# FFN and layer activations turned by VectorE and DMA instead of by TensorE, in a float32 decoder layer on one Trainium2 core

## The chip, the cores and the metric

One of the eight cores of a Trainium2 chip runs the program. The metric is the device time of one execution in microseconds (us). A core has five engines: TensorE (matmuls; PE in the profile, PEld its weight loads), VectorE (DVE), ScalarE (ACT), GpSimd (POOL) and SyncE (SP, which here only issues DMAs). Each engine takes its instructions in program order; a DMA is issued from an engine's queue and waits there for what it depends on.

## What is computed

The reference is one decoder layer over 256 positions with 2048 channels, in float32. Cut to what matters here:

```python
h = x + 0.5 * swiglu(rms_norm(x, norm_ffn1), w1_gate, w1_up, w1_down)       # D_FF = 5632
z = rms_norm(h, norm_mix) @ w_in
y = concat(rms_norm(s5_mixer(z_ssm)), rms_norm(gmlp_mixer(z_u, z_v)))
h = h + y @ w_out
h = h + 0.5 * swiglu(rms_norm(h, norm_ffn2), w2_gate, w2_up, w2_down)
h = h + sigmoid(rms_norm(h, norm_ple) @ w_ple_gate) * (p @ w_ple_proj)
return rms_norm(h, norm_final)
# swiglu(x) = (silu(x @ w_gate) * (x @ w_up)) @ w_down;  g below is the bracket
```

## The kernel before

Everything is a stream of weight products. `ffn_groups`, `mix_groups` and `ple_groups` write a plan of groups; a group is 512 output columns of one weight matrix, for both halves t of the 256 positions, summed over its blocks k of 128 rows. `stream` (L94) walks the plan in steps of two blocks, called ticks here: `load` (L108) issues a 1 MB weight load on SP for every two ticks, with three buffers `raw`; `do_split` (L117) splits a tick's weights into a high part `wh` (ScalarE, L133) and a low part `wl` (VectorE, L134), three ticks ahead of their use, with four buffers each; `products` (L138) issues the tick's 12 matmuls (2 blocks, 2 halves, 3 products at L147, L148 and L149) into a PSUM tile `acc`. A group over 2048 rows has 8 ticks, one over 5632 rows (w_down) has 22, and one over 1024 rows (w_out) has 4.

When a group's last tick is issued, its `post` is spawned and runs at once (L166 to L168). A post is a generator: `yield n` puts what follows n ticks later, so the order of every engine's queue is set by where a post stands among the ticks. The posts that matter here:

- `up_post` (L365), after each of the 11 pairs of a gate group and an up group of an FFN (one pair is 16 ticks): VectorE multiplies (L371, two instructions) into the tile `g`; then, one and two ticks later, four 128x128 blocks of g are transposed by TensorE into a PSUM tile `tr` (`transposes`, L196 to L200), and `split_plain` (L202) splits this into `gTah`/`gTal` or `gTbh`/`gTbl` (ScalarE L203, VectorE L204). These are the stationary operands of w_down.
- `down_post` (L387), after each of the four groups of w_down: VectorE adds into h (L390), ScalarE squares it (`square`, L223), and `h_to_T` (L225) transposes the 512 columns in two steps of four blocks, one and two ticks later, and splits them with the gain of the next norm (`split_gain2`, L211: ScalarE L214, VectorE L217) into `hTh`/`hTl`, the stationary operands of the next stage.
- `wo_post` (L863), after each of the four last groups of w_out: the same with L867 in place of L390.

So four blocks are transposed 44 times for g (11 pairs, 2 FFNs, 2 steps) and 24 times for h (12 chunks of 512 columns, 2 steps). Other transposes (`s5_tables`, `s5_block`, `gmlp`, `glu_post`) use the same helper.

Beside FFN1 runs `s5_tables` (L431), a long chain of small VectorE work that is paced by a budget per tick (`paced`, L67). It is cut into four quarters. In each, GpSimd clears two columns of the tile `qt` (`g.memset`, L606 and L607) right before VectorE fills the table (L608 and L525), and `put` (L527) stores it to DRAM (`stash`) by DMA. GpSimd also computes each norm's power (`rstd`, L194) and part of `s5_block` (L687). It issues no DMA.

Of the kernel before, what the change touches and what calls it, by code (L numbers as in the profile page):

```python
# [7 lines left out]
F32 = mybir.dt.float32  # L8
F32R = mybir.dt.float32r
I32 = mybir.dt.int32  # L10
AF = mybir.ActivationFunctionType
# [4 lines left out]
P = 128  # L16
# [5 lines left out]
NW = 512  # L22
# [32 lines left out]
class Layer:  # L55
# [166 lines left out]
        j = self.junk_p.tile([P, NW], F32, tag="junk", name="junk")  # L222
        self.nc.scalar.activation(out=j, in_=src, func=AF.Square, accum_out=acc)  # L223

    def h_to_T(self, n, gcol):  # L225

        for b in range(2):
            yield 1
            k0 = 4 * n + 2 * b
            ps = self.transposes(  # L230
                [self.h[:, t, (k0 + kk) * P:(k0 + kk + 1) * P] for kk in range(2) for t in range(2)])
            self.split_gain2(ps, self.gcol[:, gcol + k0:gcol + k0 + 2], self.hTh[:, k0:k0 + 2], self.hTl[:, k0:k0 + 2])
# [4 lines left out]
    def kernel(self):  # L237
        tc, nc, I = self.tc, self.nc, self.i
        pool = tc.tile_pool
        base = [pool(name="const", bufs=1), pool(name="small", bufs=2), pool(name="raw", bufs=3),  # L240
                pool(name="wh", bufs=LA_SPLIT + 1), pool(name="wl", bufs=LA_SPLIT + 1), pool(name="junk", bufs=1),
                pool(name="acc", bufs=4, space=PSUM), pool(name="aux", bufs=4, space=PSUM),
                pool(name="dram", bufs=1, space=DRAM)]
        const, self.small, self.raw_p, self.wh_p, self.wl_p, self.junk_p, self.acc_p, self.aux_p, dram = [
            p.__enter__() for p in base]
        self.gcol = const.tile([P, 96], F32, name="gcol")
        nc.scalar.dma_start(out=self.gcol, in_=I["cols"])
        self.ident = const.tile([P, P], F32, name="ident")
        make_identity(nc, self.ident)
        self.mhalf = const.tile([P, 2], F32, name="mhalf")  # L250
        nc.gpsimd.memset(self.mhalf, -0.5)
        act_warm = const.tile([P, 2], F32, name="act_warm")
        nc.scalar.activation(out=act_warm, in_=self.mhalf, func=AF.Silu)
        self.mag2 = const.tile([P, 32], F32, name="mag2")
        self.r = [const.tile([P, 2], F32, name=f"r{n}") for n in range(6)]
        self.ssq = [const.tile([P, 4, 2], F32, name=f"ssq{n}") for n in range(7)]
        self.h = const.tile([P, 2, D], F32, name="h")
        self.hTh = const.tile([P, 16, 256], F32R, name="hTh")
        self.hTl = const.tile([P, 16, 256], F32R, name="hTl")
        self.stash = dram.tile([2 * NQ, P, BW], F32, name="stash")  # L260
        self.pools, self.cms = {}, {}

        self.plan = []
        self.ffn_groups(1)
        self.mix_groups()
        self.ffn_groups(2)
        self.ple_groups()


        warm = self.aux_p.tile([P, NW], F32, tag="aux", name="warm")  # L270
        for _ in range(N_WARM):
            nc.tensor.matmul(warm[:, 0:P], self.ident, self.ident, start=True, stop=True)
        self.open("gta", "gt")
        self.open_g()
        self.open("xt", "xt")
        xt = self.pools["xt"].tile([P, 16, 256], F32, name="xt")
        self.preload, self.presplit = {}, {}

        def xt_load(a, b):
            return lambda: nc.sync.dma_start(out=xt[:, a:b, :], in_=I["xT"][:, a:b, :])  # L280

        def x_load(t):
            return lambda: nc.sync.dma_start(out=self.h[:, t, :], in_=I["x"][:, t, :])

        def xt_split(i):
            def f():
                for k in ((i,) if i < 2 else (2 * i - 2, 2 * i - 1)):
                    self.split_gain(xt[:, k, :], self.gcol[:, k:k + 1], self.hTh[:, k, :], self.hTl[:, k, :])
                if i == 8:
                    self.close("xt")  # L290
            return f
        for li, fs in {0: [xt_load(0, 1)], 1: [xt_load(1, 2)], 2: [xt_load(2, 4)], 3: [xt_load(4, 6)],
                       4: [xt_load(6, 8)], 5: [xt_load(8, 12)], 6: [xt_load(12, 16)], 7: [x_load(0)],
                       8: [x_load(1)]}.items():
            self.preload[li] = fs
        for i in range(9):
            self.presplit[i] = [xt_split(i)]

        def startup():
            yield 6  # L300
            for t in range(2):
                for n in range(4):
                    self.square(self.h[:, t, n * NW:(n + 1) * NW], self.ssq[0][:, n, t:t + 1])
                    if n % 2:
                        yield 1
            self.rstd([self.ssq[0][:, n, :] for n in range(4)], D, self.r[0])
        self.spawn(startup())
        self.spawn(self.paced(self.s5_tables()), 8)
        self.stream()
        for n in list(self.pools)[::-1]:  # L310
            self.close(n)
        for p in base[::-1]:
            p.__exit__(None, None, None)
# [11 lines left out]
    KA = 24  # L325

    def open_g(self):
        self.gT_a = (self.pools["gta"].tile([P, self.KA, 256], F32R, name="gTah"),
                     self.pools["gta"].tile([P, self.KA, 256], F32R, name="gTal"))
        self.open("gs", "gs", 2)  # L330

    def open_gb(self):
        self.open("gtb", "gtb")
        n = 44 - self.KA
        self.gT_b = (self.pools["gtb"].tile([P, n, 256], F32R, name="gTbh"),
                     self.pools["gtb"].tile([P, n, 256], F32R, name="gTbl"))

    def gT_at(self, k):
        if k < self.KA:
            return self.gT_a, k  # L340
        return self.gT_b, k - self.KA

    def ffn_groups(self, which):
        I = self.i
# [19 lines left out]
        def up_post(c):  # L364
            def post(g):  # L365
                gt = st.pop(c)
                if which == 1 and c == 6:
                    self.close("wrk")
                    self.open_gb()
                for t in range(2):  # L370
                    self.nc.vector.scalar_tensor_tensor(  # L371
                        out=gt[t], in0=g.ps[t], scalar=r[:, t:t + 1], in1=gt[t], op0=ALU.mult, op1=ALU.mult)
                for b in range(2):
                    yield 1
                    ps = self.transposes(
                        [gt[t][:, (2 * b + kk) * P:(2 * b + kk + 1) * P] for kk in range(2) for t in range(2)])
                    (th, tl), k = self.gT_at(4 * c + 2 * b)
                    self.split_plain(ps, th[:, k:k + 2, :].rearrange("p a b -> p (a b)"),
                                     tl[:, k:k + 2, :].rearrange("p a b -> p (a b)"))
            return post  # L380

        def act_g(k, t):
            (th, tl), kk = self.gT_at(k)
            return th[:, kk, t * P:(t + 1) * P], tl[:, kk, t * P:(t + 1) * P]

        def down_post(n):
            def post(g):  # L387
                for t in range(2):
                    hs = self.h[:, t, n * NW:(n + 1) * NW]
                    self.nc.vector.scalar_tensor_tensor(  # L390
                        out=hs, in0=g.ps[t], scalar=0.5, in1=hs, op0=ALU.mult, op1=ALU.add)
                ssq = self.ssq[1 if which == 1 else 5]
                for t in range(2):
                    self.square(self.h[:, t, n * NW:(n + 1) * NW], ssq[:, n, t:t + 1])
                if n == 3:
                    self.rstd([ssq[:, i, :] for i in range(4)], D, self.r[1 if which == 1 else 4])
                yield from self.h_to_T(n, 16 if which == 1 else 48)
            return post

        for c in range(11):  # L400
# [393 lines left out]
    def mix_groups(self):  # L794
# [68 lines left out]
        def wo_post(n, rr, ssm):  # L863
            def post(g):
                for t in range(2):
                    hs = self.h[:, t, n * NW:(n + 1) * NW]
                    nc.vector.scalar_tensor_tensor(out=hs, in0=g.ps[t], scalar=rr[:, t:t + 1], in1=hs,  # L867
                                                   op0=ALU.mult, op1=ALU.add)
                if not ssm:
                    return  # L870
                for t in range(2):
                    self.square(self.h[:, t, n * NW:(n + 1) * NW], self.ssq[4][:, n, t:t + 1])
                if n == 3:
                    self.rstd([self.ssq[4][:, i, :] for i in range(4)], D, self.r[3])
                yield from self.h_to_T(n, 32)
            return post

        def glu_post(n):
# [218 lines left out]
```

## Time and profile before

| | us |
|---|---|
| three runs, median | 1879.89 (1879.21 to 1880.82) |
| the profiled execution, its own time | 1880.12 |
| the span of its instructions in the trace | 1878.4 |
| granted TensorE clock over the span | 0.999 of full speed |

The profile is one execution. Its page gives the busy time of each engine, the chain of work that ended last (followed back from the last instruction, at each step to what released it), the costliest groups of instructions by line, engine and tile, and the DMA issues. The trace can also be asked for the instructions in order of time, for waits, and for busy time by stretch. Matmuls are pipelined: a row's duration is longer than the time from its start to the next one's start.

### The profile page before, as it was taken

To read this page: it belongs to the slowest core of one execution; us is meant where nothing else is said; L and a number is where in the kernel's file an instruction comes from. 1 tells how busy PE (TensorE), PEld (TensorE's weight loads), DVE (VectorE), ACT (ScalarE), POOL (GpSimd) and SP (SyncE) were. 2 spreads that over 40 slices of the span, in tenths; PEclk is the share of its full clock that TensorE was granted. 3 is DMA by queue.
4 is the path that set the end of the run, shared out by engine and by line. 5 is a ranking of instruction groups with operands and counts; after the bars stand their busy time and mean duration, and the time that the engine had idled before them with its cause. 6 is when DMAs were issued, how large, how long until landed. Compare 5 with 4: busy or idle time off the path is not lost.

```text
span 1878.4 us, 21983 instructions
## 1 busy us (share of the span) xinstructions
PE 1866.7 (99%) x8752; PEld 1549.8 (83%) x8752; DVE 1115.5 (59%) x1519; ACT 845.4 (45%) x1018; POOL 45.9 (2%) x58
## 2 busy tenths in 40 slices
PE   9999999999999999999999999999999999999998
PEld 7888888888888888888888888888888888888887
DVE  6788886545545554698876555555445555455565
ACT  6444444444434443444455544444444444344454
POOL 1000000000000000022100000000000000000000
PEclk9999999999999999999999999999999999999999
DMA  8566666555455555565545555555555555555553
GB/s 323 202 212 236 236 214 225 195 182 199 179 199 182 195 186 199 216 255 210 185 175 179 186 198 182 194 186 181 198 182 198 181 195 186 199 182 194 193 202 134
DMA packets 62535, 373.64 MB, mean 199 GB/s; under 512 B 7777, under 2 KB 13153, under 8 KB 19809
## 3 DMA queue, kind: packets, MB, share of 16 engines
q1 hardware_dynamic: 62000, 371.67, 55.0%
q8 instruction: 68, 1.11, 0.2%
q10 hardware_dynamic: 432, 0.57, 0.1%
q14 instruction: 35, 0.28, 0.0%
HBM read 360.55 MB, written 11.53 MB: 198 GB/s over the span
## 4 chain that ended last, share of the span: by engine, by line
PE 98%; DMA 1%; DVE 0%; ACT 0%; SPq 0%; issue 0%; POOLq 0%; DVEq 0%; ACTq 0%
PE acc L147 31%; PE acc L149 31%; PE acc L148 31%; PE tr L199 2%; PE y L726 1%; DMA raw<-in_w_gate 1%; PE v L679 0%; PE sp L767 0%; PE mps L590 0%; PE y L720 0%; DVE wl L134 0%; ACT wh L133 0%; PE late L149 0%; PE late L148 0%; PE late L147 0%; SPq L280 0%
## 5 line engine op out<-in xcount | busy, mean ns | idle before, releaser
L134 DVE TENSOR_TENSOR wl<-raw,wh 128x1024 fp32r<-128x1024 f32 (+1 forms) x649 | 802.4, 1238 | 662.1 <-ACT wh L133 658.9
L133 ACT ACTIVATE wh<-raw 128x1024 fp32r<-128x1024 f32 (+1 forms) x649 | 686.1, 1058 | 771.5 <-PE acc L149 741.7
L147 PE MATMUL acc<-wh,hTh 128*128 128x512 f32 (+1 forms) x1744 | 684.8, 393 | 0.0
L148 PE MATMUL acc<-wl,hTh 128*128 128x512 f32 (+1 forms) x1744 | 678.4, 389 | 1.4 <-DVE wl L134 1.4
L149 PE MATMUL acc<-wh,hTl 128*128 128x512 f32 (+1 forms) x1744 | 679.1, 389 | 0.0
L149 PEld LDWEIGHTS acc<-wh,hTl 128*128 128x128 f32 x1744 | 327.3, 188 | 68.6
L148 PEld LDWEIGHTS acc<-wl,hTh 128*128 128x128 f32 x1744 | 327.6, 188 | 68.2 <-DVE wl L134 2.1
L147 PEld LDWEIGHTS acc<-wh,hTh 128*128 128x128 f32 x1744 | 327.5, 188 | 66.8 <-ACT wh L133 0.3
L147 PE MATMUL acc<-wh,gTah 128*128 128x512 f32 x384 | 150.9, 393 | 0.0
L149 PE MATMUL acc<-wh,gTal 128*128 128x512 f32 x384 | 149.7, 390 | 0.0
L148 PE MATMUL acc<-wl,gTah 128*128 128x512 f32 x384 | 149.5, 389 | 0.0
L147 PE MATMUL acc<-wh,gTbh 128*128 128x512 f32 x320 | 124.5, 389 | 0.0
L148 PE MATMUL acc<-wl,gTbh 128*128 128x512 f32 x320 | 124.5, 389 | 0.0
L149 PE MATMUL acc<-wh,gTbl 128*128 128x512 f32 x320 | 124.5, 389 | 0.0
L149 PEld LDWEIGHTS acc<-wh,gTal 128*128 128x128 f32 x384 | 72.1, 188 | 15.2
L148 PEld LDWEIGHTS acc<-wl,gTah 128*128 128x128 f32 x384 | 72.1, 188 | 14.6
L147 PEld LDWEIGHTS acc<-wh,gTah 128*128 128x128 f32 x384 | 72.1, 188 | 14.5
L147 PEld LDWEIGHTS acc<-wh,gTbh 128*128 128x128 f32 x320 | 60.1, 188 | 12.5
L149 PEld LDWEIGHTS acc<-wh,gTbl 128*128 128x128 f32 x320 | 60.1, 188 | 12.5
L148 PEld LDWEIGHTS acc<-wl,gTbh 128*128 128x128 f32 x320 | 60.1, 188 | 12.4
L360 ACT ACTIVATE g<-acc,r 128x512 f32<-128x512 f32 x44 | 29.9, 689 | 19.8 <-PE acc L149 19.8
L194 POOL TENSOR_TENSOR r<-rs,mhalf 128x2 f32<-128x2 f32 x6 | 5.1, 856 | 1355.0 <-DVE rs L193 1343.8
(228 smaller groups left out, 1051.5 us busy)
## 6 DMA issues: line engine op xcount, KB each, us to landing
raw<-in_w_up SPq DMA_DIRECT2D x88, 1024.0 KB, 4.8
raw<-in_w_down SPq DMA_DIRECT2D x88, 1024.0 KB, 4.8
raw<-in_w_gate SPq DMA_DIRECT2D x86, 1024.0 KB, 4.8
raw<-in_w_in SPq DMA_DIRECT2D x24, 1024.0 KB, 4.8
raw<-in_w_out SPq DMA_DIRECT2D x16, 1024.0 KB, 4.8
raw<-in_w_ple_gate SPq DMA_DIRECT2D x16, 1024.0 KB, 4.8
qt<-stash SPq DMA_DIRECT2D x8, 1152.0 KB, 5.3
stash<-qt SPq DMA_DIRECT2D x8, 640.0 KB, 4.7
```

Source lines behind the costliest of these rows:

```text
L133: nc.scalar.activation(out=wh[:, 0:nk, :], in_=src, func=AF.Copy)
L134: nc.vector.tensor_tensor(out=wl[:, 0:nk, :], in0=src, in1=wh[:, 0:nk, :].bitcast(F32), op=ALU.subtract)
L147: nc.tensor.matmul(o, ah, wh[:, j, c0:c1], start=first, stop=False)
L148: nc.tensor.matmul(o, ah, wl[:, j, c0:c1], start=False, stop=False)
L149: nc.tensor.matmul(o, al, wh[:, j, c0:c1], start=False, stop=last)
L194: nc.gpsimd.tensor_tensor(out=out, in0=s2, in1=self.mhalf, op=ALU.pow)
L199: self.nc.tensor.transpose(ps[:, i * P:(i + 1) * P], b, self.ident)
L360: self.nc.scalar.activation(out=st[c][t], in_=g.ps[t], func=AF.Silu, scale=r[:, t:t + 1])
L726: nc.tensor.matmul(ps[:, 64 * i:64 * i + 64], R[ri][:, i, :], qt[:, f0:f0 + 64], start=False, stop=(a == 1 and ri == 1))
```

## The change

A new method `flip` takes the place of the TensorE transposes for all of g (22 chunks of 512 columns) and for 8 of the 12 chunks of h: in each FFN the chunks n = 0, 1, 2 of the four of w_down, and after w_out the chunks n = 0 and 2. The other four chunks of h (and all other transposes) stay on TensorE.

`flip` has VectorE transpose all 32x32 blocks of a chunk (two instructions of 128x512) into one new SBUF tile `tr` of 128x1024, which leaves the blocks in the wrong partitions. A DMA on GpSimd's queue writes `tr` to a DRAM tile `gsc` (512 KB; two of them in turn), and four DMAs on the same queue read it back into `tr`, one for each 32 partitions (128 KB each, in runs of 256 numbers), so that every block lands in its partitions. The four wait for the write. There is one `tr`, used by all flips. The post then yields 6 ticks before the split is issued, in place of one and two ticks. For g, the split is one ScalarE and one VectorE instruction over 128x1024, read from SBUF in runs of 32 numbers. For h, ScalarE scales `tr` in place by the gain (four instructions of 128x256) and copies it to `hTh` (two of 128x512), and VectorE subtracts (two of 128x512). The pool `gs` of the tile g goes from two buffers to one, and the g operands are stored by chunk, so `act_g` picks 128 columns from another place.

```diff
--- before.py
+++ after.py
@@ -222,8 +222,21 @@
         j = self.junk_p.tile([P, NW], F32, tag="junk", name="junk")
         self.nc.scalar.activation(out=j, in_=src, func=AF.Square, accum_out=acc)
 
-    def h_to_T(self, n, gcol):
-
+    def h_to_T(self, n, gcol, flip):
+
+        if flip:
+            tr = self.flip([self.h[:, t, n * NW:(n + 1) * NW] for t in range(2)])
+            yield 6
+            for kk in range(4):
+                v = tr.rearrange("p (i t kk u) -> p kk (i t) u", i=4, t=2, kk=4)[:, kk]
+                self.nc.scalar.activation(out=v, in_=v, func=AF.Copy, scale=self.gcol[:, gcol + 4 * n + kk:gcol + 4 * n + kk + 1])
+            dh, dl = (y[:, 4 * n:4 * n + 4, :].rearrange("p kk (t i u) -> p t kk i u", t=2, i=4) for y in (self.hTh, self.hTl))
+            trv = tr.rearrange("p (i t kk u) -> p t kk i u", i=4, t=2, kk=4)
+            for t in range(2):
+                self.nc.scalar.activation(out=dh[:, t], in_=trv[:, t], func=AF.Copy)
+            for t in range(2):
+                self.nc.vector.tensor_tensor(out=dl[:, t], in0=trv[:, t], in1=dh[:, t].bitcast(F32), op=ALU.subtract)
+            return
         for b in range(2):
             yield 1
             k0 = 4 * n + 2 * b
@@ -258,6 +271,9 @@
         self.hTh = const.tile([P, 16, 256], F32R, name="hTh")
         self.hTl = const.tile([P, 16, 256], F32R, name="hTl")
         self.stash = dram.tile([2 * NQ, P, BW], F32, name="stash")
+        self.gsc = [dram.tile([P, 4 * 256], F32, name=f"gsc{b}") for b in range(2)]
+        self.spot = 0
+        self.tr = const.tile([P, 4 * 256], F32, name="tr")
         self.pools, self.cms = {}, {}
 
         self.plan = []
@@ -325,20 +341,37 @@
     KA = 24
 
     def open_g(self):
-        self.gT_a = (self.pools["gta"].tile([P, self.KA, 256], F32R, name="gTah"),
-                     self.pools["gta"].tile([P, self.KA, 256], F32R, name="gTal"))
-        self.open("gs", "gs", 2)
+        n = self.KA // 4
+        self.gT_a = (self.pools["gta"].tile([P, n, 4 * 256], F32R, name="gTah"),
+                     self.pools["gta"].tile([P, n, 4 * 256], F32R, name="gTal"))
+        self.open("gs", "gs")
 
     def open_gb(self):
         self.open("gtb", "gtb")
-        n = 44 - self.KA
-        self.gT_b = (self.pools["gtb"].tile([P, n, 256], F32R, name="gTbh"),
-                     self.pools["gtb"].tile([P, n, 256], F32R, name="gTbl"))
-
-    def gT_at(self, k):
-        if k < self.KA:
-            return self.gT_a, k
-        return self.gT_b, k - self.KA
+        n = 11 - self.KA // 4
+        self.gT_b = (self.pools["gtb"].tile([P, n, 4 * 256], F32R, name="gTbh"),
+                     self.pools["gtb"].tile([P, n, 4 * 256], F32R, name="gTbl"))
+
+    def gT_at(self, c):
+        if c < self.KA // 4:
+            return self.gT_a, c
+        return self.gT_b, c - self.KA // 4
+
+    def flip(self, src):
+
+
+
+        nc, tr = self.nc, self.tr
+        trv = tr.rearrange("p (a t kk u) -> p t kk a u", a=4, t=2, kk=4)
+        for t in range(2):
+            nc.vector.transpose(out=trv[:, t], in_=src[t].rearrange("p (kk a u) -> p kk a u", kk=4, a=4))
+        sc = self.gsc[self.spot]
+        self.spot ^= 1
+        nc.gpsimd.dma_start(out=sc, in_=tr)
+        sv = sc.rearrange("(i f) (a x) -> a f i x", i=4, a=4)
+        for a in range(4):
+            nc.gpsimd.dma_start(out=tr[32 * a:32 * a + 32, :].rearrange("f (i x) -> f i x", i=4), in_=sv[a])
+        return tr
 
     def ffn_groups(self, which):
         I = self.i
@@ -370,18 +403,18 @@
                 for t in range(2):
                     self.nc.vector.scalar_tensor_tensor(
                         out=gt[t], in0=g.ps[t], scalar=r[:, t:t + 1], in1=gt[t], op0=ALU.mult, op1=ALU.mult)
-                for b in range(2):
-                    yield 1
-                    ps = self.transposes(
-                        [gt[t][:, (2 * b + kk) * P:(2 * b + kk + 1) * P] for kk in range(2) for t in range(2)])
-                    (th, tl), k = self.gT_at(4 * c + 2 * b)
-                    self.split_plain(ps, th[:, k:k + 2, :].rearrange("p a b -> p (a b)"),
-                                     tl[:, k:k + 2, :].rearrange("p a b -> p (a b)"))
+                (th, tl), k = self.gT_at(c)
+                tr = self.flip(gt)
+                yield 6
+                self.split_plain(tr.rearrange("p (i b u) -> p b i u", i=4, b=8),
+                                 th[:, k, :].rearrange("p (b i u) -> p b i u", b=8, i=4),
+                                 tl[:, k, :].rearrange("p (b i u) -> p b i u", b=8, i=4))
             return post
 
         def act_g(k, t):
-            (th, tl), kk = self.gT_at(k)
-            return th[:, kk, t * P:(t + 1) * P], tl[:, kk, t * P:(t + 1) * P]
+            x, c = self.gT_at(k // 4)
+            m = P * (4 * t + k % 4)
+            return tuple(y[:, c, m:m + P] for y in x)
 
         def down_post(n):
             def post(g):
@@ -394,7 +427,7 @@
                     self.square(self.h[:, t, n * NW:(n + 1) * NW], ssq[:, n, t:t + 1])
                 if n == 3:
                     self.rstd([ssq[:, i, :] for i in range(4)], D, self.r[1 if which == 1 else 4])
-                yield from self.h_to_T(n, 16 if which == 1 else 48)
+                yield from self.h_to_T(n, 16 if which == 1 else 48, n < 3)
             return post
 
         for c in range(11):
@@ -872,7 +905,7 @@
                     self.square(self.h[:, t, n * NW:(n + 1) * NW], self.ssq[4][:, n, t:t + 1])
                 if n == 3:
                     self.rstd([self.ssq[4][:, i, :] for i in range(4)], D, self.r[3])
-                yield from self.h_to_T(n, 32)
+                yield from self.h_to_T(n, 32, n % 2 == 0)
             return post
 
         def glu_post(n):
```

## Rows read from the trace of the kernel before

**Rows 1.** The page: the span, and busy time of each engine.

```profile
span 1878.4 us, 21983 instructions
PE 1866.7 (99%) x8752; PEld 1549.8 (83%) x8752; DVE 1115.5 (59%) x1519; ACT 845.4 (45%) x1018; POOL 45.9 (2%) x58
```

**Rows 2.** The page: the chain that ended last, by engine.

```profile
PE 98%; DMA 1%; DVE 0%; ACT 0%; SPq 0%; issue 0%; POOLq 0%; DVEq 0%; ACTq 0%
```

**Rows 3.** Timeline of PE around a transpose group: start us, us, what.

```profile
299.74 0.39 PE L149 MATMUL acc<-wh,hTl 128*128 128x512 f32 x1
...
331.70 0.39 PE L149 MATMUL acc<-wh,hTl 128*128 128x512 f32 x1
331.93 0.60 PE L199 MATMUL tr<-ident,g 128*128 128x128 f32 x4
...
332.60 0.40 PE L148 MATMUL acc<-wl,hTh 128*128 128x512 f32 x1
```

**Rows 4.** Timeline of DVE: posts one chunk apart, in FFN1 and in its w_down.

```profile
373.41 1.40 DVE L371 SCALAR_TENSOR_TENSOR g<-acc,r,g 128x512 f32<-128x512 f32 x2
417.91 1.40 DVE L371 SCALAR_TENSOR_TENSOR g<-acc,r,g 128x512 f32<-128x512 f32 x2
...
567.71 1.28 DVE L390 SCALAR_TENSOR_TENSOR h<-acc,h 128x512 f32<-128x512 f32 x2
628.52 1.28 DVE L390 SCALAR_TENSOR_TENSOR h<-acc,h 128x512 f32<-128x512 f32 x2
```

**Rows 5.** Groups by line, shapes kept apart: count, busy us, mean ns, idle before.

```profile
L134 DVE TENSOR_TENSOR wl<-raw,wh 128x1024 fp32r<-128x1024 f32 x647 | 801.0, 1239 | 659.7 <-ACT wh L133 656.5
L199 PE MATMUL tr<-ident,g 128*128 128x128 f32 x176 | 26.4, 272 | 0.0
L217 DVE SCALAR_TENSOR_TENSOR hTl<-tr,gcol,hTh 128x256 fp32r<-128x256 f32 x48 | 21.0, 480 | 13.3 <-ACT hTh L214 12.4
L214 ACT ACTIVATE hTh<-tr,gcol 128x256 fp32r<-128x256 f32 x48 | 20.1, 471 | 22.5 <-PE tr L199 22.5
L687 POOL TENSOR_TENSOR te<-te,tf 128x512 f32<-128x512 f32 x8 | 17.2, 2147 | 0.0
L204 DVE TENSOR_TENSOR gTal<-tr,gTah 128x512 fp32r<-128x512 f32 x24 | 16.5, 688 | 15.3 <-ACT gTah L203 15.3
L199 PE MATMUL tr<-ident,h 128*128 128x128 f32 x96 | 14.4, 272 | 0.0
L702 DVE TENSOR_TENSOR_SCAN tb<-mag,ta 128x128 f32<-128x128 f32 x32 | 12.8, 401 | 0.0
L687 POOL TENSOR_TENSOR ta<-ta,tb 128x512 f32<-128x512 f32 x8 | 10.3, 1288 | 102.5 <-DVE tb L684 89.5 <-issue 13.0
L1019 DVE TENSOR_SCALAR hg<-hg,r 128x512 f32<-128x512 f32 x6 | 2.6, 484 | 1.4 <-POOL r L1013 1.4
```

**Rows 6.** Timeline of ACT in FFN1: start us, us, what, idle before it.

```profile
393.91 1.06 ACT L133 ACTIVATE wh<-raw 128x1024 fp32r<-128x1024 f32 x1 [1.66 <-PE acc L149]
```

**Rows 7.** Source L114, the SP queue: ns min/median/max of an issue.

```profile
L114 SPq DMA_DIRECT2D raw<-in_w_up x88: 327/328/1119, 16.4 to 1501.9; - x88
DMA to landing us min/median/max: 3.2/4.8/11.4
```

**Rows 8.** The page: a DMA issue of `put`, KB, us to landing.

```profile
stash<-qt SPq DMA_DIRECT2D x8, 640.0 KB, 4.7
```

**Rows 9.** Busy time by stretch: PE, PEld, DVE, ACT, POOL, PEclk, DMA share, GB/s.

```profile
146.00:192.00 46.00, 46.00 (x238) 38.11 (x237) 38.73 (x92) 19.59 (x22) 0.15 (x2) 1.00 0.68 237
373.00:418.00 45.00, 45.00 (x204) 37.23 (x203) 22.82 (x22) 19.20 (x20) 0.00 (x0) 1.00 0.54 194
```

**Rows 10.** Timeline of DVE: flip site and the table's first fill after it.

```profile
99.31 1.40 DVE L371 SCALAR_TENSOR_TENSOR g<-acc,r,g 128x512 f32<-128x512 f32 x2
...
117.18 0.18 DVE L608 COPY qt<-C 128x8 f32<-128x8 f32 x1
```

**Rows 11.** Timeline of SP in FFN1: one weight load's issue.

```profile
393.54 0.33 SPq L114 DMA_DIRECT2D raw<-in_w_up  x1
```

## The prediction, made before the change was run

> **What bounds the kernel now.** I read the page from the top. The engines' busy times come first: TensorE is busy 1866.7 of 1878.4 us, VectorE 59%, ScalarE 45%, GpSimd 2% [rows 1]. A busy share alone does not say which engine sets the end, so the chain that ended last comes next: 98% of it is TensorE's own work, one matmul behind the other [rows 2]. An instruction taken off TensorE's queue therefore comes off the time, as long as nothing that replaces it makes TensorE wait. To price one I read the timeline of TensorE around a transpose group. 141 matmuls lie between the starts at 299.74 and 331.70, so a matmul takes a place of 31.96 / 141 = 0.2267 us, though its row says 0.39 [rows 3]; a tick of 12 has 2.72 us. The last matmul before a group of four transposes starts at 331.70 and the second one after it at 332.60. Without the group these would be two places apart, so the group holds TensorE for 0.90 - 0.45 = 0.45 us.
>
> The same price from a longer stretch: two posts of neighbouring pairs lie 417.91 - 373.41 = 44.50 us apart, and 16 ticks of 12 matmuls fill 192 x 0.2267 = 43.52; the two groups between them cost 0.98, or 0.49 each. In w_down two posts lie 60.81 apart and 22 ticks fill 59.84: 0.97, or 0.485 each [rows 4]. The matmuls behind a group are slightly spread as well, and that is what the longer stretch adds. I take 0.485.
>
> **What goes.** The 176 transposes of g [rows 5] are 44 groups. Of the 96 of h [rows 5], in 24 groups, 8 chunks of 12 go: 16 groups. Together 60 x 0.485 = 29.1 us, all of it on the chain. At the near price of 0.45 it would be 27.0. The end of the kernel and its start are not touched.
>
> **VectorE and ScalarE.** For a chunk of g, VectorE loses two splits of 0.69 us and gets one over 1024 columns, whose nearest row is `wl` with 1.24, and two block transposes of 512 columns [rows 5]. No row shows a block transpose. The cheapest 512-column instruction from SBUF took 0.48 us, and a scan over 128 columns 0.40, so 1.6 for 512 [rows 5]; I take 0.69, by the 512-column rows that pass one number after another. So 1.24 + 1.38 - 1.38 = +1.24 us in 43.5. In the middle of FFN1 VectorE is busy 22.8 of 45 us; beside the tables it is 38.7 of 46 [rows 9], and 1.24 more still fits. ScalarE swaps two splits for one as long as `wh`, 1.06 [rows 6]. A chunk of h swaps four splits of 0.48 on VectorE for four of about 0.69 (two of them transposes), and on ScalarE keeps four of 0.47 [rows 5] and adds two copies over 512 columns, about 0.7 each (between 0.47 for 256 and 1.06 for 1024). None of this is on the chain: `wh` of a tick starts when TensorE frees a buffer, after 1.66 us of idle time [rows 6], three ticks ahead of its use. If that cover were gone, each us would count 30 times.
>
> **The wait that is added.** Behind each flip stand its write, its four reads and, six ticks later, the split. Count time from the end of the group's last matmul, T. The multiply takes 1.4 us [rows 4] and the transposes 1.4: the write can be issued at 2.8. GpSimd issues no DMA before. SP's issue takes 0.33, at most 1.12 [rows 7], so five would be 1.65; I take that, since it is the same kind of instruction, and keep as the other end five of GpSimd's longest kind, 2.15 each or 10.7 in all [rows 5]. The nearest transfers: `put` stores 640 KB in 4.7 [rows 8], and a load of 1 MB lands in 4.8 [rows 7], so 9.5 for the two hops. The reads land at about 2.8 + 1.65 + 9.5 = 14.0; with GpSimd's price at 23.0.
>
> When must they? The split is queued on ScalarE behind `wh` for tick 8, which ends about 13.6 + 1.1 = 14.7 us after T, so at 14.0 it does not even stop ScalarE. If it does, `wh` and `wl` for tick 9 are what is late: from the landing L on come 1.06 (split), 1.24 (VectorE's half, beside `wh`) and 1.24 (`wl`), 3.6 with the hand-overs, and tick 9 begins at 24.5. TensorE waits when L is above about 21.0; for h the ScalarE part is 4 x 0.47 + 2 x 0.7 = 3.3, with `wh` and `wl` behind it, and the limit about 19. That leaves 7 and 5 us to spare, and I cost the wait at nothing. The operands themselves are wanted later still, the tightest after w_out, n = 2, at tick 8 (21.8): L + 3.3 + 0.7 is 18.0.
>
> **Other queues.** GpSimd stands still until the write has landed, and behind it wait its own few instructions. The one that VectorE needs is the clearing of `qt` before a table is filled: the first fill comes 117.18 - 99.31 = 17.9 us after a flip's site [rows 10], the other three later in their pair, and GpSimd has issued its reads by about 9. SP's queue gets nothing new. The one tile `tr` is free 10 ticks before the next flip of g, and 2 ticks (less about 4 us of splits) after w_out's n = 0. Losing one buffer of `gs` costs nothing: the next Silu is 8 ticks away.
>
> **The transfer's pattern.** `put` moves runs of 256 numbers too, and 640 KB of them landed in 4.7 us [rows 8], so I price the rearranged read like an ordinary one. The Trainium skill speaks against it (VectorE: DVE Perf Modes, section on the three transpose paths): a plain copy whose strides do the transposing, with a large innermost stride, is 19 times slower than the DMA's own transpose. By that the two hops would be an estimated 19 x 4.8 = 91 us, each flip some 75 us late, and the kernel at over twice its time; `put`'s row does not agree, and I see the reason in its run length.
>
> **Sum.** 1880.1 - 29.1 = 1851.0 us against the profiled execution, whose own time lies 0.2 above the median of the three runs. I forecast 1851, with 1849.5 to 1854 as this case's own range (0.45 to 0.51 us for a group).
>
> **Rival 1, slower: GpSimd is late with its DMAs.** GpSimd's adds over 128x512 took 1.29 us in one place and 2.15 on average in the other, with the same shape [rows 5]: something holds it up while VectorE is busy beside it. If that happens to each of the five issues, L is 23.0: 2.0 late for 22 chunks of g and 4 for 8 of h, or 76 us, and the time 1851 + 76 = 1927. It decides from about 1 us late per flip, L near 22. Against it: nearest rows give 14, and an issue of 2 us is six times SP's. The Trainium skill has this as a rule (SBUF — State Buffer, section on SBUF's two separate sides): a GpSimd-queue DMA whose descriptors are blocked by VectorE's two-port operations took 3.1 us instead of 0.62. By that estimate five DMAs would be 12.4 us later, L 26, and the time near 2020. No row here shows a DMA of GpSimd, so it cannot be checked. The case's VectorE work beside the flips is `wl`, at 1.21 ns a column no fast mode [rows 5], so nothing of that kind runs there for long. Chance 0.11.
>
> **Rival 2: VectorE falls behind beside the tables.** There it is busy 38.7 of 46 us [rows 9]. At a flip's site, 1.4 of multiply, 1.4 of transposes, 1.24 of `wl` and about 0.9 of table work meet in a tick of 2.72; with transposes at 1.6 each it is 4 us over, and `wl` has some 5.9 of lead. Five pairs run beside the tables; if each loses 2 us, the time is 1861. Chance 0.06.
>
> **Rival 3: the flips hold up the weights.** A flip moves 1 MB through engines that are busy 54 to 68% [rows 9]. A load issued at 393.54 [rows 11] is split from about 404.8 on, and lands after 4.8, so 6.5 us are spare; a whole load's time more leaves 1.7. Only with the longest landing, 11.4 [rows 7], is a split late. If each flip cost half a us: 1866. Chance 0.06. That the transposes stay on TensorE after all is excluded by the diff; 0.02 stay for what I do not see, 0.75 for the forecast.
>
> **How the numbers follow.** A measurement of this kernel can tell about 0.2% from no change, 3.8 us. Faster: 0.75 + 0.06 + most of rival 3, 0.85. Slower: rival 1, 0.11. Within 0.2%: 0.04, for partial lateness of some 0.9 us a flip. The range takes in the forecast's own and rival 2, 1849.5 to 1863; of rival 3 its milder half, and nothing of rival 1.
>
> **What would show it.** Right: no `tr` written from g, 32 instead of 96 from h; posts of neighbouring pairs 43.5 us apart in FFN2 instead of 44.5; ScalarE's split of g waiting little or not at all on the DMA; no wait of TensorE for `wl`. A landing later than 21 us after the multiply, with TensorE idle in tick 9, would prove rival 1; waits of `wl` inside FFN1's first five pairs alone rival 2; ScalarE waiting for `raw` rival 3. If the pairs come to 43.5 and the sum is still short, the price of a group was wrong.

## The result and the profile after

The changed kernel takes 1850.45 us (1850.1 to 1851.49, four runs) against 1879.86 before: a ratio of 0.9844 (95% interval 0.9832 to 0.9856). The forecast was 1851.0. The profiled execution took 1851.49 us.

The page of the changed kernel, busy times and the chain by engine, to set beside [rows 1, 2]:

```profile
span 1849.8 us, 21900 instructions
PE 1837.9 (99%) x8512; PEld 1526.8 (83%) x8512; DVE 1140.3 (62%) x1541; ACT 854.5 (46%) x1012; POOL 131.0 (7%) x208
...
PE 98%; DMA 1%; issue 1%; DVE 0%; ACT 0%; SPq 0%; POOLq 0%; POOL 0%; DVEq 0%; ACTq 0%
```

TensorE has 8752 - 8512 = 240 matmuls less, which is 60 groups of four, and 28.8 us less busy time; the span is 28.6 shorter. TensorE is still 98% of the chain.

The groups by line of the changed kernel, shapes apart, for what is new and for the transposes that stay:

```profile
L373 POOL DMA_DIRECT2D tr<-gsc x120 | 65.5, 552 | 97.4 <-DMA gsc<-tr 91.2 <-ACT wh L133 3.6 <-issue 2.6
L367 DVE STREAM_TRANSPOSE tr<-g 128x512 f32<-128x512 f32 x44 | 28.5, 685 | 0.0
L370 POOL DMA_DIRECT2D gsc<-tr x30 | 17.0, 568 | 1160.1 <-DVE tr L367 1160.1
L204 DVE TENSOR_TENSOR gTal<-tr,gTah 128x1024 fp32r<-128x1024 f32 x12 | 14.7, 1224 | 4.1 <-ACT gTah L203 3.9
L203 ACT ACTIVATE gTah<-tr 128x1024 fp32r<-128x1024 f32 x12 | 12.7, 1060 | 8.4 <-DMA tr<-gsc 8.4
L236 ACT ACTIVATE hTh<-tr 128x512 fp32r<-128x512 f32 x16 | 9.2, 624 | 0.3
...
L199 PE MATMUL tr<-ident,h 128*128 128x128 f32 x32 | 4.8, 272 | 0.0
```

No `tr` comes from g on TensorE any more, and 32 instead of 96 from h [rows 5]. A block transpose over 512 columns takes 0.685 us on VectorE (taken: 0.69), an issue on GpSimd 0.55 to 0.57 (taken: 0.33, other end 2.15). Before the first read of a flip GpSimd stands until the write has landed, 91.2 us in all for 29 of the 30 flips.

The timeline of VectorE in the changed kernel, at the places of [rows 4]:

```profile
367.03 1.40 DVE L404 SCALAR_TENSOR_TENSOR g<-acc,r,g 128x512 f32<-128x512 f32 x2
...
410.55 1.40 DVE L404 SCALAR_TENSOR_TENSOR g<-acc,r,g 128x512 f32<-128x512 f32 x2
...
617.27 1.28 DVE L423 SCALAR_TENSOR_TENSOR h<-acc,h 128x512 f32<-128x512 f32 x2
677.11 1.28 DVE L423 SCALAR_TENSOR_TENSOR h<-acc,h 128x512 f32<-128x512 f32 x2
```

A pair lasts 43.52 us instead of 44.50, and a chunk of w_down 59.84 instead of 60.81: what 192 and 264 matmuls fill at 0.2267 us each. Nothing is lost in between.

One flip of the changed kernel, first on GpSimd, then on ScalarE (timelines; in brackets the idle time before and what ended it):

```profile
369.94 0.56 POOL L370 DMA_DIRECT2D gsc<-tr  x1 [37.54 <-DVE tr L367]
374.09 2.18 POOL L373 DMA_DIRECT2D tr<-gsc  x4 [3.59 <-ACT wh L133]
...
381.12 1.06 ACT L133 ACTIVATE wh<-raw 128x1024 fp32r<-128x1024 f32 x1 [1.66 <-PE acc L149]
383.38 1.06 ACT L203 ACTIVATE gTbh<-tr 128x1024 fp32r<-128x1024 f32 x1 [1.20 <-DMA tr<-gsc]
384.34 1.04 ACT L133 ACTIVATE wh<-raw 128x1024 fp32r<-128x1024 f32 x1
386.56 1.06 ACT L133 ACTIVATE wh<-raw 128x1024 fp32r<-128x1024 f32 x1 [1.17 <-PE acc L149]
```

The write goes out 2.9 us after the post at 367.0 (forecast 2.8), the reads between 7.1 and 9.2, and the split starts at 383.4, so the reads landed 16.3 us after the post where 14.0 was forecast. (The wait of 3.59 us before these reads is the one of the 30 that the profile puts down to ScalarE; for the other 29 it names the write.) ScalarE waits 1.2 us for them and has made it up two `wh` later: the one at 386.56 waits for TensorE again, as in [rows 6].

Waits in the changed kernel: engine, line waited for, us in total, times, longest.

```profile
ACT wh L133 <- DMA raw<-in_w_up: 13.9, 5, 7.3
...
ACT gTah L203 <- DMA tr<-gsc: 8.4, 8, 2.7
...
ACT gTbh L203 <- DMA tr<-gsc: 5.4, 5, 2.1
```

13 of the 22 splits of g wait a little. And beside the tables ScalarE waits for weights three times, once for 7.3 us, which it did not do there before: the beginning of rival 3. None of it reaches TensorE, which waits 1.3 us in all for `wl` (1.4 before).

### The profile page after: what moved, and what is told of

Same layout as the page of the kernel before. It is cut to its first block, busy times and chain, and to the rows that moved or that the text cites. A ratio compares the mean times of both kernels' runs of the same rounds, so it can differ in the third digit from the quotient of the medians.

```text
span 1849.8 us, 21900 instructions
## 1 busy us (share of the span) xinstructions
PE 1837.9 (99%) x8512; PEld 1526.8 (83%) x8512; DVE 1140.3 (62%) x1541; ACT 854.5 (46%) x1012; POOL 131.0 (7%) x208
## 4 chain that ended last, share of the span: by engine, by line
PE 98%; DMA 1%; issue 1%; DVE 0%; ACT 0%; SPq 0%; POOLq 0%; POOL 0%; DVEq 0%; ACTq 0%
PE acc L147 32%; PE acc L149 32%; PE acc L148 32%; PE tr L199 1%; PE y L759 1%; DMA raw<-in_w_gate 1%; PE v L712 0%; PE sp L800 0%; PE mps L623 0%; PE y L753 0%; DVE wl L134 0%; ACT wh L133 0%; SPq L296 0%; DVE hg L1052 0%; DVE h L1035 0%
## 5 line engine op out<-in xcount | busy, mean ns | idle before, releaser
L370 POOL DMA_DIRECT2D gsc<-tr x30 | 17.0, 568 | 1160.1 <-DVE tr L367 1160.1
L373 POOL DMA_DIRECT2D tr<-gsc x120 | 65.5, 552 | 97.4 <-DMA gsc<-tr 91.2
L148 PEld LDWEIGHTS acc<-wl,gTbh 128*128 128x128 f32 x320 | 60.1, 188 | 12.5
```

The costliest lines, as they stand in the source:

```text
L148: nc.tensor.matmul(o, ah, wl[:, j, c0:c1], start=False, stop=False)
L370: nc.gpsimd.dma_start(out=sc, in_=tr)
L373: nc.gpsimd.dma_start(out=tr[32 * a:32 * a + 32, :].rearrange("f (i x) -> f i x", i=4), in_=sv[a])
```

## The experiments

`g_only`, `h_only` and `g_only_sp` ran four times each, all other variants once; executions of the kernel before lie within 2.1 us of each other in all these comparisons.

**The two parts alone.** `g_only` leaves h on TensorE, `h_only` leaves g there:

```diff
-                yield from self.h_to_T(n, 16 if which == 1 else 48, n < 3)
+                yield from self.h_to_T(n, 16 if which == 1 else 48, False)
-                yield from self.h_to_T(n, 32, n % 2 == 0)
+                yield from self.h_to_T(n, 32, False)
```

`h_only` is the kernel before with the new `h_to_T` and `flip` alone.

> Theory (each group of four transposes costs TensorE 0.485 us and the flips cost nothing): 44 groups go, 1879.9 - 21.3 = 1858.5 us, within 1 us. Rival (the flips of h cost something, for instance the eight that share TensorE's stage with the squares of h, and g's gain pays for it): below 1857.

> Theory: 16 groups go, 1879.9 - 7.8 = 1872.1 us, within 1 us, so that the two parts add up to the whole change. Rival: the chunks of h lose part of it to their longer ScalarE work or to the limit that is 2 us nearer, 1874 or more.

`h_only` took 1871.98 us (ratio 0.9959, interval 0.9944 to 0.9974) against 1879.65, a gain of 7.7 where 7.8 was expected. `g_only` took 1862.49 (0.9908, 0.9892 to 0.9925): 17.2 gained, not 21.3. Its posts follow each other at the expected 43.52 us, and the last post of w_down comes 1769.49 - 1747.58 = 21.9 us earlier than before. The missing 4 us are behind it. The instructions of the program's last line, first in `g_only`, then in the changed kernel (ns min/median/max, first and last start):

```profile
L1125 POOLq DRAIN  x3: 40/102/9670, 1850.1 to 1860.2; - x3
L1125 SPq DRAIN  x3: 7/7/7, 1855.5 to 1860.0; - x3
```

```profile
L1125 POOLq DRAIN  x3: 40/102/4280, 1843.2 to 1849.5; - x3
L1125 SPq DRAIN  x3: 7/7/7, 1848.6 to 1848.9; - x3
```

After its last computation (1850.1 in `g_only`) GpSimd's queue drains for 9.67 us, to 1859.8. SP has seen the output land at 1855.5 and everything else waits for GpSimd. In the changed kernel the drain lasts 4.28, to 1847.5, and the output lands later, at 1848.6, so it is covered. Two runs put this to the test.

> g alone is flipped, as in the run that kept 4 us of the forecast's gain, but its DMAs go out on SP's queue. Theory (those 4 us are GpSimd's last instruction, a drain of 9.67 us at the program's end that outlasts the output's transfers, and it comes from GpSimd's DMAs): the drain is back at 0.65 us and the time at the forecast's 1858.5, within 1. Rival (the flips of g themselves lose 4 us when h stays on TensorE): 1862 to 1863 again.

`g_only_sp` has `nc.sync` for `nc.gpsimd` in the two `dma_start` lines of `flip`. It took 1858.40 (0.9886, 0.987 to 0.9903), the forecast's number for g; the drain is at 0.65 us. The flips of g lose nothing.

> 26 flips, 130 DMAs on GpSimd: g, two chunks of h in FFN1 and two after w_out. TensorE's part by 52 groups: 1879.9 - 25.2 = 1854.7. GpSimd's last drain took 3.96 us with 8 flips, 9.67 with 22, 4.28 with 30 and 4.69 with 31. Theory A (0.41 us for each flip since a point that lies between 22 and 26 flips): 2.7 us, and 1854.7. Theory B (that point lies behind 26): 11.3 us, about 6 more than the output's transfers cover, and 1860 to 1861.

```diff
-                yield from self.h_to_T(n, 16 if which == 1 else 48, n < 3)
+                yield from self.h_to_T(n, 16 if which == 1 else 48, n < 2 and which == 1)
```

1854.15 us, and the drain 2.65: theory A, to 0.1 us in the drain and 0.6 us in the time. From 8 to 22 flips it grows by (9.67 - 3.96) / 14 = 0.41 us a flip, from 26 to 30 by (4.28 - 2.65) / 4 = 0.41, and with 31 (the run `h3_too` below) it is 4.69; between 22 and 26 it falls back and starts anew. What GpSimd does in this time no run shows.

**How near the wait is.** In `delay4` and `delay3` the two `yield 6` are 4 and 3:

```diff
             tr = self.flip([self.h[:, t, n * NW:(n + 1) * NW] for t in range(2)])
-            yield 6
+            yield 4
...
                 tr = self.flip(gt)
-                yield 6
+                yield 4
```

> The split is queued four ticks after the flip in place of six. Theory (TensorE waits when the last read lands later than the delay plus three ticks, less 3.6 us for a chunk of g and 5.4 for one of h): the limits are 15.4 and 13.6 us, and the reads of the changed kernel land 13.5 to 16.5 after the post; a loss of some 0.2 us a flip of g and 0.5 to 1 of h, 1853 to 1864. Rival (the operands are wanted much later, so the split's place does not matter): 1850.5.

> Three ticks in place of six. Theory: the limits are 12.7 and 10.9 us, each flip of g about 2 us late and each of h about 3: 1850.5 + 44 + 24 = 1918, within 1895 to 1940, with TensorE idle before the matmuls on a late wh or wl. Rival: 1850.5, and ScalarE's wait for the read is all that grows.

1880.65 and 1963.28 us, both beyond what was expected: the wait reaches TensorE, but at 4 ticks not mainly where it was looked for. Posts of neighbouring pairs of FFN2 stay at 43.5 to 44.2 us in `delay4`; over all its flips the reads land 12.5 to 19.4 us after the post, 15.3 in the middle, at g's limit of 15.4. Of the 30 us some 10 come beside the tables of FFN1, 6.5 of them in the one pair whose reads land at 19.4, and 2 in FFN2. 16.6 come after w_out: from its first post with a flip to its last post 50.2 us pass, and 33.6 in the changed kernel. TensorE's timeline there, with the idle time before:

```profile
1019.66 0.48 PE L199 MATMUL tr<-ident,h 128*128 128x128 f32 x1 [6.68 <-DVE h L900]
1020.32 0.90 PE L199 MATMUL tr<-ident,h 128*128 128x128 f32 x3 [0.18 <-DVE h L900]
...
1049.94 0.48 PE L199 MATMUL tr<-ident,h 128*128 128x128 f32 x1 [5.59 <-DVE h L900]
```

ScalarE and VectorE before the first of these gaps:

```profile
1015.25 1.70 ACT L232 ACTIVATE tr<-tr,gcol 128x256 f32<-128x256 f32 x4 [6.61 <-DMA tr<-gsc]
...
1017.64 1.29 DVE L238 TENSOR_TENSOR hTl<-tr,hTh 128x512 fp32r<-128x512 f32 x2 [7.75 <-ACT hTh L236]
1018.86 1.40 DVE L900 SCALAR_TENSOR_TENSOR h<-acc,r,h 128x512 f32<-128x512 f32 x2
```

A chunk of w_out is 4 ticks long. With a delay of 4, the split of one chunk (L238) is queued ahead of the addition into h of the next (L900) on VectorE, and it waits for the reads; TensorE's transposes of that next chunk wait for the addition. The delay of 6 lets the addition go first. The two gaps are 12.3 of the 16.6 us; behind them the granted clock is 0.63 and 0.54 on the mean of 4 us (1020 to 1024 and 1050 to 1054).

In `delay3` the waits of TensorE are of the kind that was forecast:

```profile
PE acc L147 <- ACT wh L133: 33.4, 25, 6.7
PE acc L148 <- DVE wl L134: 25.4, 30, 1.0
PE tr L199 <- DVE h L900: 14.2, 4, 7.0
```

That is 73 us of idle time out of 113 lost. TensorE's busy time is 40 us longer for the same 8512 matmuls (1878.1 against 1837.9 us); the mean granted clock is 0.981 over the span where it was 0.998. That the clock makes up all of these 40 us is likely but not shown.

**Where the queue stands.** In `sp_queue`, `act_queue` and `sp_delay3` `nc.sync` or `nc.scalar` takes the place of `nc.gpsimd` in `flip`; in `sp_delay3` both delays are 3 as well:

```diff
-        nc.gpsimd.dma_start(out=sc, in_=tr)
+        nc.sync.dma_start(out=sc, in_=tr)
...
-            nc.gpsimd.dma_start(out=tr[32 * a:32 * a + 32, :].rearrange("f (i x) -> f i x", i=4), in_=sv[a])
+            nc.sync.dma_start(out=tr[32 * a:32 * a + 32, :].rearrange("f (i x) -> f i x", i=4), in_=sv[a])
```

> The five DMAs of a flip are issued on SP's queue, with the weight loads. Theory: SP stands in the queue from the post until the write has landed and the reads are out, about 8 us; the load that would be issued 3.8 us after the post is about 4 us late, within its 6.5 us of slack outside the tables' stretch: 1850 to 1854, with ScalarE waiting more often for raw. Rival (the weight loads have no such slack, and that is why a queue of its own is needed): 1860 or more.

> The same five DMAs on ScalarE's queue. Theory: ScalarE stands from the post until the reads are out, 7 to 8 us, so wh and wl of the third tick end near 10 us where TensorE wants them at 8.4: about 2 us lost a flip, 1850.5 + 60 = 1910, within 1885 to 1935. Rival (only the transfers' length matters, not whose queue waits): 1850 to 1854, as on SP.

> The split three ticks after the flip, which cost 113 us with GpSimd's DMAs, with the DMAs on SP's queue. Theory (what is late are GpSimd's reads, which land 15 to 16 us after the post; on SP the write takes 2.6 and a read 2.9 after issues of 0.33, so the last read lands at 3 + 3 + 1.3 + 3, some 10 to 11, below the limit of 12.7 for g): 1851 to 1858. Rival (the two hops through DRAM need 15 us from whichever queue): 1940 or more.

`sp_queue` took 1850.73: SP stands 148.8 us for the transposes and 71.7 for the writes, the weights come later by that, and their slack takes it. The kernel before ran at 1878.77 beside it. `act_queue` took 1892.76, 42 us more for the same transfers, where some 60 were expected. ScalarE's timeline at a flip of it:

```profile
1091.49 1.06 ACT L133 ACTIVATE wh<-raw 128x1024 fp32r<-128x1024 f32 x1 [1.66 <-PE acc L149]
1096.37 0.34 ACTq L370 DMA_DIRECT2D gsc<-tr  x1
1099.03 1.77 ACTq L373 DMA_DIRECT2D tr<-gsc  x4
1101.17 3.91 ACT L133 ACTIVATE wh<-raw 128x1024 fp32r<-128x1024 f32 x4 [8.62 <-issue]
```

ScalarE does nothing for 8.6 us, until the reads are out; four `wh` have to be made up, and `wl` behind them is late: 1.4 us lost a flip on the average.

`sp_delay3` took 1860.36, about 2 us above the expected range. All its splits of g start 9.7 to 12.1 us after the post. Its DMAs, and the same on GpSimd's queue in the changed kernel (KB each, median us to landing):

```profile
gsc<-tr SPq DMA_DIRECT2D x30, 512.0 KB, 2.6
tr<-gsc SPq DMA_DIRECT2D x120, 128.0 KB, 3.0
```

```profile
gsc<-tr POOLq DMA_DIRECT2D x30, 512.0 KB, 3.2
tr<-gsc POOLq DMA_DIRECT2D x120, 128.0 KB, 4.4
```

So the last read lands 5 us sooner from SP's queue, and below g's limit even at three ticks, where GpSimd's cost 113 us. Of the 10 us that are left, 8 are once more w_out: from its first flip to the second 26.6 us (23.1 in the changed kernel), and 59.8 from there to FFN2's first post (55.1). The order on VectorE is the same there: L238 stands ahead of L900, and TensorE's transposes wait 4.3 us for L900 in all.

**VectorE beside GpSimd's issue.** `vec_copies` puts six copies on VectorE right behind the transposes of g; nothing uses them.

```diff
                 tr = self.flip(gt)
+                j = self.junk_p.tile([P, NW], F32, tag="junk", name="junk")
+                for _ in range(6):
+                    self.nc.vector.tensor_copy(out=j, in_=self.h[:, 0, 0:NW])
```

> Six copies of 128x512 from SBUF to SBUF on VectorE right behind each flip of g; they leave nothing that is used. Theory: GpSimd's issue of the write stays at 0.56 us, since only its own instructions hold it; VectorE is about 2 us later, inside its lead of 5.9: 1850 to 1854. Rival (the Trainium skill, SBUF: State Buffer: VectorE's two-port copies keep GpSimd from writing descriptors, 3.1 us in place of 0.62): the write's issue grows to between 1.5 and 3 us where the copies run beside it, and the time stays below 1856 even so, since 2 us fit under the limit. Second rival (VectorE's backlog beside the tables): 5 flips lose 2 us or more, 1860.

1850.80 us. VectorE and GpSimd in its timeline at one flip, and GpSimd's group for the write:

```profile
368.91 2.70 DVE L410 COPY junk<-h 128x512 f32<-128x512 f32 x6
371.52 3.49 DVE L134 TENSOR_TENSOR wl<-raw,wh 128x1024 fp32r<-128x1024 f32 x3
...
369.29 0.59 POOL L370 DMA_DIRECT2D gsc<-tr  x1 [37.84 <-DVE tr L367]
...
L370 POOL DMA_DIRECT2D gsc<-tr x30 | 17.9, 598 | 1161.2 <-DVE tr L367 1100.9 <-DVE junk L410 60.3
```

The write's issue lies wholly inside the copies and takes 0.59 us; the mean of all 30 goes from 568 to 598 ns, and the write lands after 3.0 us in the median (3.2 in the changed kernel). The copies take 0.45 us each, against 0.69 for the 512-column instructions that pass one number after another. Three `wl` are made up in a row here, and the pairs beside the tables take no longer together than in the changed kernel. Both rivals fall: neither GpSimd's issue nor VectorE's backlog matters here. One thing does move: a read lands after 5.9 us in the median instead of 4.4, though the last one of a flip in FFN2 still lands 15 to 17 us after the post. Why, no run shows.

**A chunk without cover.** `h3_too` flips the last chunk of FFN1's w_down as well (`n < 3 or which == 1`).

> The last chunk of FFN1's w_down is flipped too, whose operands the next stage wants at its tick 6, 16.3 us after the post. Theory: 0.97 us go, and TensorE waits at the matmuls of block 12 for the landing plus 3.9 us, that is 1.5 to 4 us: 1851 to 1854, and the wait is to be seen in the trace. Rival (the four tiles are wanted no sooner than the others): no wait, 1849.5.

1854.46 us, half a us above the expected range and some 4 more than the two full variants that ran beside it (1850.73 and 1850.80), where 0.97 would have been gained. TensorE's timeline at block 12 of the next stage:

```profile
752.16 0.39 PE L148 MATMUL acc<-wl,hTh 128*128 128x512 f32 x1
752.39 0.39 PE L149 MATMUL acc<-wh,hTl 128*128 128x512 f32 x1
756.35 0.80 PE L147 MATMUL acc<-wh,hTh 128*128 128x512 f32 x1 [3.57 <-ACT hTh L236]
756.94 0.63 PE L148 MATMUL acc<-wl,hTh 128*128 128x512 f32 x1
757.36 0.63 PE L149 MATMUL acc<-wh,hTl 128*128 128x512 f32 x1
...
759.07 0.47 PE L147 MATMUL acc<-wh,hTh 128*128 128x512 f32 x1
759.38 0.40 PE L148 MATMUL acc<-wl,hTh 128*128 128x512 f32 x1
```

It waits 3.6 us, as expected, and then starts its next matmuls 0.43 us apart in place of 0.227, for about 2.7 us. The busy time by stretch (PE, PEld, DVE, ACT, POOL, granted clock, DMA share, GB/s):

```profile
752.00:756.00 4.00, 0.78 (x4) 0.32 (x2) 0.42 (x1) 2.04 (x5) 0.00 (x0) 0.98 0.52 209
756.00:760.00 4.00, 3.65 (x10) 2.92 (x11) 2.52 (x3) 1.77 (x3) 0.00 (x0) 0.60 0.00 0
760.00:764.00 4.00, 4.00 (x20) 3.29 (x19) 1.23 (x1) 2.23 (x3) 0.00 (x0) 1.00 0.92 354
```

The granted clock is 0.60 on the mean of the stretch behind the gap: half speed, 1.2 GHz, for most of it. The idle time is paid once as a wait and a second time at the lower clock.

## Why the prediction was right

**The price of a group, 0.485 us.** Right. The chunks' lengths and the two parts (7.7 for 16 groups; 21.5 for 44 in `g_only_sp`) agree with it, and they add up to 29.2 of the 29.4 us gained.

**VectorE and ScalarE at nothing.** Right: the block transpose was sized to 1%. No row had shown one, so this was a choice between 0.48 and 1.6; but the six copies add 2.7 us a flip of g and left the time where it was, so a transpose of 1.6 would not have shown either.

**The wait at nothing, with 7 us to spare.** Right in the result, too generous in the landing. It was forecast at 14.0 us, with 0.33 an issue and 4.8 for the read; measured were 0.55 an issue and, at most flips of g, a landing 15 to 16 us after the post. One flip beside the tables landed at 18.7: its last read goes out 8.1 us after the post and needs 10.6. The mis-sized term is the reads' hop on GpSimd's queue: in the flip shown above the last read needs 7.5 us, while the write needs 3.6 where 4.7 was forecast. Why GpSimd's last read takes so long stays open. Of the 7 us to spare 5 to 6 were there at most flips, and 2 at that one. The limit itself held for g within about half a us: in `delay4`, where it was put at 15.4, FFN2's reads at 16.0 cost their pair less than 0.1 us, and those at 16.2 and 16.6 cost 0.3 and 0.7; at three ticks the pairs of FFN2 lose 1.5 to 4.7 us.

**What stands behind the split on VectorE** was not in the prediction. It named what waits behind GpSimd's DMAs and behind ScalarE's split, and for w_out the operands' due time alone. There it is the order of the split and the next addition into h that decides, and the delay of 6 that keeps it; that the forecast of no wait came true at this place is luck, since its reasoning did not look there. The due time had less room as well: the operands of w_out's second flip were ready 20.4 us after the post, where 18.0 was forecast and 21.8 allowed.

**Rival 1** needed a landing near 22. GpSimd's issue is 0.55, and neither it nor the write's landing is slowed by VectorE's copies. The rule of the Trainium skill that was set beside it (SBUF — State Buffer, on its two separate sides) is not seen here: 0.59 us, not 3.1, inside copies that take 0.45 us for 512 columns each.

**Rival 2** did not come about: the first six intervals between the posts of FFN1, which hold the tables, take 5.9 us less together, 0.98 each like the others. **Rival 3** began (a wait of 7.3 us for weights, landings of up to 12.2 instead of 11.4) and stayed within the slack. The Trainium skill's factor of 19 for a rearranged plain copy with a large innermost stride (VectorE: DVE Perf Modes, on the three transpose paths) is not seen with these runs of 256 numbers: a read lands after 4.4 us in the median from GpSimd's queue and 3.0 from SP's.

**The start and the end "not touched".** Right for the changed kernel by 1.1 us only: GpSimd's final drain ends at 1847.5 and the output's landing covers it until 1848.6.

## What to carry to other kernels

An operation on the engine that is busy 99% is worth its place in the queue (start to start), not its duration, and can be traded for a slow detour of 15 us if that detour is queued where nobody waits behind it. Before choosing a delay, list for each engine what will stand behind the delayed instruction, the next step's first instruction above all; the same transfers cost 0, 42 or 113 us here by queue and delay (`sp_queue`, `act_queue`, `delay3`). And look at the program's last line when a new queue is used: its drain can hold the end.

## What was not expected of the hardware

GpSimd's queue drains at the end for 0.65 us without DMAs of its own, and for 2.65 to 9.67 with them: 0.41 us more for each five DMAs, starting anew between 110 and 130 of them. A gap of 3.6 us on TensorE brought half the granted clock for about 2.7 us behind it (0.60 on the mean of 4 us). A read of 128 KB from DRAM, one of four in a row, landed after 4.4 us in the median from GpSimd's queue and 3.0 from SP's.
